# Forget attention: three of its four q and k projection chunks with the weight blocks stationary, a bank per block

## The chip, the cores and the metric

One core of a Trainium2 chip runs the whole program. The metric is the device time of one execution in microseconds (us). A core has a matrix engine (PE), VectorE (DVE), ScalarE (ACT), GpSimd (POOL) and the queues that start transfers (SP among them). Each engine works through its own row of instructions in order; between engines an instruction waits for a semaphore. A matmul multiplies a stationary block, loaded into the array first, with a moving operand of up to 512 columns, and writes into a bank of PSUM (128 partitions by 512 numbers of 32 bits). There are eight banks. ACT and DVE read a bank; when they have read it, it can be used again.

## What is computed

Four layers with different attention, each between two feed-forward layers, and then a second block. The change lies in the second layer's attention alone, the forget attention, over 256 positions with 16 heads of 64:

```
def fox_mixer(x, w_in, b_f, w_out):
    d = MIX_WIDTH                                   # 1024
    q, k, v, f = jnp.split(x @ w_in, [d, 2 * d, 3 * d], axis=-1)
    ...
    log_f = jax.nn.log_sigmoid(f.astype(jnp.float32) + b_f.astype(jnp.float32))
    cum = jnp.transpose(jnp.cumsum(log_f, axis=1), (0, 2, 1))
    o = causal_block_attention(q, k, v, HEAD_DIM ** -0.5, cum)
    return o.reshape(B, S, d) @ w_out

def causal_block_attention(q, k, v, scale, cum=None):
    for i in range(S // Q_BLOCK):                   # two blocks of 128 queries
        lo, hi = i * Q_BLOCK, (i + 1) * Q_BLOCK
        s = jnp.einsum('bqhd,bkhd->bhqk', q[:, lo:hi], k[:, :hi]) * scale
        s = s + cum[:, :, lo:hi, None] - cum[:, :, None, :hi]
        mask = jnp.arange(lo, hi)[:, None] >= jnp.arange(hi)[None, :]
        p = jax.nn.softmax(jnp.where(mask, s, -jnp.inf), axis=-1)
        outs.append(jnp.einsum('bhqk,bkhd->bqhd', p, v[:, :hi]))
```

## The kernel before

The 256 positions are two tiles of 128 (`T` = 0 and 1). Weights come in pieces of 128 by 1024 (512 KB). SP loads a piece into one of five `raw` buffers, ACT rounds it to `whi` (`part_of`, recorded at line 242, where all of ACT's work is recorded), and DVE writes the rest to `wlo` (line 250, where nearly all of DVE's work is recorded). There are eight pairs of `whi` and `wlo`. A product of two 32-bit matrices is made of three matmuls: high by high, high by low, low by high.

A projection can be computed in two ways.

- `Chunk` (three passes, lines 417 to 419): 512 columns of the weights are the moving operand, and a block of the activations (`xt`, already transposed) is stationary. A chunk has four pieces with two blocks of 128 rows each, so for each `T` 24 matmuls of 512 columns go into one bank of the tag `acc`, of which there are two. The four pieces are read for `T` = 0 and again for `T` = 1, and each is given back (`release`) in the second reading.
- `Turned` (lines 426 and 428): a block of 128 by 128 of the weights is stationary, and the activations move. The high part meets both halves of all positions in 512 columns, the low part only the high half in 256 columns, into the bank's upper half. The result is transposed: columns of the weights on partitions, all 256 positions along the row. `whole` drains a bank: ACT copies the upper half to a buffer `h`, and DVE adds the lower half to it. Before, only feed-forward layers use it, two blocks of columns at a time in two banks, with weights in groups of two pieces.

The forget attention (`fox`) needs q and k transposed, with the 64 numbers of a head on partitions. Before, all its projections are a `Chunk`. Per chunk of q or k and per `T`, ACT copies the bank to a natural tile `g` (q scaled by 0.125), PE transposes it in four blocks (`turn8`, line 449, `ps<-ident,g`), and ACT copies the four to another `g`.

The chunks run in this order: q of the first eight heads, two small chunks with v of these heads and the forget gates, k of the first heads; then q and k of the other eight heads, and their v. When the gates are out, `cumsum` makes log-sigmoids on ACT and DVE (buffers `zf`) and sums them over positions with six small matmuls (lines 976 to 985). The attention of the first heads (`attend`) runs as threads beside the later projections, and that of the second heads beside the output projection. For a group of heads: score products (line 701), a bias made of mask and gates on DVE (`h<-mask,cq,pc`), a masked maximum out of the bank (line 713), exponentials on ACT (`wk<-wk,small`), reciprocals and scalings on DVE, four transposes of the weights of attention (line 449, `ps<-ident,wk`), a copy, and value products (line 758).

What stands where on an engine is fixed when the program is built. `Model` keeps an estimated clock for each engine (`run_on`, `pe`), and `tick` starts a step of a thread when the estimate says that it is ready; a scheduler then places the instructions with estimates of its own. On the chip the order does not change, and an instruction whose input is late holds up all that stands behind it on its engine.

## Time and profile before

| what | us |
|---|---|
| median of three runs | 2404.85 (2404.65 to 2406.1) |
| the profiled execution, its own time | 2409.01 |
| its span in the trace | 2407.2 |
| PE busy | 2385.8 |
| DVE busy | 1703.9 |
| ACT busy | 1302.5 |

All times in the trace count from the start of the span. The forget attention's projections lie between about 702 and 789 us, the first changed chunk begins at 728.47, and the next feed-forward layer at 819.45. A matmul's row shows when it began and how long it was in the array; matmuls overlap, so what one costs is the distance between the starts of neighbours. In the rows `ps` is a bank, and `g`, `h`, `wk`, `zf` are buffers of the kinds named above.

### The profile page before, as it was taken

The page shows a single profiled execution, that of the slowest core. Times are in us where ns is not written, and L with a number is a line of the kernel's source. Part 1 is how long each engine was busy: PE and PEld are TensorE (multiplying, and loading weights), DVE is VectorE, ACT ScalarE, POOL GpSimd, SP SyncE. Part 2 cuts the span into 40 slices and gives each one's busy share as a digit, 9 for nine tenths or more (in the row PEclk, how much of TensorE's full clock was granted, in tenths as well). Part 3 has the DMA queues.
Part 4 walks back from the last instruction along what each step waited for, and adds up shares of the span by engine and source line. Part 5 has one row for each costly group of instructions (what it writes and reads, how often), then busy time and mean ns, then how long its engine had stood idle before and what let it go on. Part 6 is the DMA issues. An engine that isn't in the chain of part 4 may idle for free. (4 is left out here: it accounts for less than half of the span.)

```text
span 2407.2 us, 35665 instructions
## 1 busy us (share of the span) xinstructions
PE 2385.8 (99%) x13007; PEld 2010.5 (84%) x13007; DVE 1703.9 (71%) x3265; ACT 1302.5 (54%) x2226; POOL 80.6 (3%) x123
## 2 busy tenths in 40 slices
PE   9999999999999999999999999999999999999998
PEld 7888888888888888888887888888778887888887
DVE  6668876576567866766678877657888767896664
ACT  5555655545456555455475554554655446744553
POOL 0000000000000000000000010000000000000000
PEclk9999999999999999999999999999999999999999
DMA  8555445555656456565454575555545655454552
GB/s 275 195 173 191 156 166 191 178 199 193 201 157 219 154 199 195 176 215 185 130 184 158 196 216 201 189 196 171 185 149 198 201 196 192 158 171 165 195 187 103
DMA packets 126481, 442.81 MB, mean 184 GB/s; under 512 B 14944, under 2 KB 17040, under 8 KB 126304
## 3 DMA queue, kind: packets, MB, share of 16 engines
q1 hardware_dynamic: 117792, 413.49, 51.4%
q0 software_dynamic: 7760, 26.05, 3.6%
q8 instruction: 102, 1.67, 0.3%
q10 hardware_dynamic: 752, 0.98, 0.1%
q14 instruction: 75, 0.61, 0.1%
HBM read 434.14 MB, written 5.80 MB: 183 GB/s over the span
## 5 line engine op out<-in xcount | busy, mean ns | idle before, releaser
L250 DVE TENSOR_TENSOR wlo<-raw,whi 128x1024 fp32r<-128x1024 f32 (+4 forms) x806 | 945.4, 1192 | 237.5 <-ACT whi L242 167.7
L242 ACT ACTIVATE whi<-raw 128x1024 fp32r<-128x1024 f32 (+4 forms) x806 | 821.1, 1031 | 307.2 <-PE ps L419 246.3
L426 PE MATMUL ps<-xt,whi 128*128 128x512 f32 x2496 | 629.1, 392 | 0.7 <-DVE h L250 0.6
L426 PEld LDWEIGHTS ps<-xt,whi 128*128 128x128 f32 x2496 | 451.9, 189 | 85.7 <-DVE h L250 2.9
L428 PEld LDWEIGHTS ps<-xt,wlo 128*128 128x128 f32 x2496 | 342.8, 190 | 25.8
L428 PE MATMUL ps<-xt,wlo 128*128 128x256 f32 x2496 | 350.8, 282 | 0.0
L417 PE MATMUL ps<-whi,g 128*128 128x512 f32 x866 | 339.5, 392 | 0.0
L418 PE MATMUL ps<-wlo,g 128*128 128x512 f32 x866 | 337.7, 390 | 0.0
L419 PE MATMUL ps<-whi,g 128*128 128x512 f32 x866 | 337.0, 389 | 0.0
L417 PE MATMUL ps<-whi,xt 128*128 128x512 f32 (+3 forms) x848 | 329.6, 389 | 4.1 <-ACT whi L242 1.9
L419 PE MATMUL ps<-whi,xt 128*128 128x512 f32 (+3 forms) x848 | 321.1, 379 | 0.6 <-DVE xt L250 0.5
L418 PE MATMUL ps<-wlo,xt 128*128 128x512 f32 (+3 forms) x848 | 319.9, 377 | 0.0
L242 ACT ACTIVATE h<-ps 128x256 f32<-128x256 f32 x352 | 117.4, 376 | 358.4 <-PE ps L428 323.3
L250 DVE TENSOR_TENSOR h<-ps,h 128x256 f32<-128x256 f32 x320 | 122.7, 419 | 218.9 <-ACT h L242 218.5
L419 PEld LDWEIGHTS ps<-whi,g 128*128 128x128 f32 x866 | 162.7, 188 | 34.4 <-DVE g L250 0.4
L417 PEld LDWEIGHTS ps<-whi,g 128*128 128x128 f32 x866 | 162.9, 188 | 31.3
L418 PEld LDWEIGHTS ps<-wlo,g 128*128 128x128 f32 x866 | 163.0, 188 | 30.2
L417 PEld LDWEIGHTS ps<-whi,xt 128*128 128x128 f32 x848 | 159.7, 188 | 32.8 <-ACT whi L242 2.3
L419 PEld LDWEIGHTS ps<-whi,xt 128*128 128x128 f32 x848 | 159.5, 188 | 31.1 <-DVE xt L250 2.0
L418 PEld LDWEIGHTS ps<-wlo,xt 128*128 128x128 f32 x848 | 159.9, 189 | 25.6
L242 ACT ACTIVATE g<-ps 128x512 f32<-128x512 f32 (+6 forms) x192 | 91.8, 492 | 94.7 <-PE ps L419 59.1
L242 ACT ACTIVATE h<-h 128x256 f32<-128x256 f32 x144 | 60.1, 418 | 135.7 <-DVE h L250 135.7
(222 smaller groups left out, 1955.5 us busy)
## 6 DMA issues: line engine op xcount, KB each, us to landing
raw<-in_f SPq DMA_DIRECT2D x526, 512.0 KB, 4.5
raw<-in_ff SPq DMA_DIRECT2D x64, 512.0 KB, 4.6
raw<-in_dsa_qkv SPq DMA_DIRECT2D x48, 512.0 KB, 4.9
raw<-in_w_in SPq DMA_DIRECT2D x40, 512.0 KB, 4.7
raw<-in_wo SPq DMA_DIRECT2D x32, 512.0 KB, 4.4
gb<-in_ln POOLq DMA_DIRECT2D x22, 512.0 KB, 4.7
raw<-in_fox_qk SPq DMA_DIRECT2D x16, 512.0 KB, 5.0
raw<-in_dsa_idx SPq DMA_DIRECT2D x16, 292.0 KB, 3.5
```

The costliest lines, as they stand in the source:

```text
L242: self.pin(self.nc.scalar.activation(out, in_, func, **kw))
L250: self.pin(getattr(self.nc.vector, fn)(out, *a, **kw))
L417: mm(acc, x[0], w[0], start=start, stop=False)
L418: mm(acc, x[0], w[1], start=False, stop=False)
L419: mm(acc, x[1], w[0], start=False, stop=stop)
L426: mm(acc, w, x.rearrange("p z t q->p (z t q)"), start=first, stop=False)
L428: mm(acc[:, S:], w, x[:, 0].rearrange("p t q->p (t q)"), start=False, stop=last)
```

## The change

Three of the four q and k chunks become a `Turned`: k of the first heads, and q and k of the other heads. The first q chunk stays. Each chunk has four blocks of 128 columns. A block has a bank `acc` of its own (where feed-forward layers take two), and its weights are taken in one group of four pieces: eight matmuls of 512 columns with the high parts, then eight of 256 with the low parts. `whole` drains a block into half of a `g` tile, with q's factor 0.125 now in both of its steps. The transposes of these chunks, and ACT's copies around them, are gone. `heads` finds two heads' rows in a block; they lie on partitions as the score product wants them.

```
 class Turned:
-    def __init__(self, m, npieces, kpp, width, x, pairs, post):
+    def __init__(self, m, npieces, kpp, width, x, pairs, post, group=2):
...
-        self.pieces, self.group = [None] * npieces, 2
+        self.pieces, self.group = [None] * npieces, group
...
-            acc = m.ybanks("tr" if j % 2 else "acc")
+            acc = [m.bank("acc")] if len(pair) == 1 else m.ybanks("tr" if j % 2 else "acc")
...
-    def whole(self, out, b, t):
+    def whole(self, out, b, t, scale=1.0):
         half = self.h([P, S])
-        t = self.A(half, b.v[:, S:], AF.Copy, after=t)
-        t = self.V("tensor_tensor", out, b.v[:, :S], half, op=OP.add, after=t)
+        t = self.A(half, b.v[:, S:], AF.Copy, scale=scale, after=t)
+        if scale != 1.0:
+            t = self.V("scalar_tensor_tensor", out, b.v[:, :S], scale, half, op0=OP.mult, op1=OP.add, after=t)
+        else:
+            t = self.V("tensor_tensor", out, b.v[:, :S], half, op=OP.add, after=t)
...
     def heads(self, fut, T, i):
-        l = fut[T]
+        pairs = isinstance(fut, Pairs)
+        l = fut[i // 4] if pairs else fut[T]
...
+            d = slice(64 * (i % 2), 64 * (i % 2) + 64)
+            r.put(l.v[d, i // 2 % 2, T * P:(T + 1) * P] if pairs else l.v[d, i // 2], l.t)
...
+    def turned_chunk(self, xf, kind, dst):
+        tiles = {}
+        def post(c, acc, t):
+            if c % 2 == 0:
+                tiles[c // 2] = self.g([P, 2, S])
+            t = self.whole(tiles[c // 2][:, c % 2], acc[0], t, 0.125 if kind == 0 else 1.0)
+            if c % 2:
+                dst[c // 2].put(tiles[c // 2], t)
+        return Turned(self, 4, 2, 512, lambda T, k: xf[T][k], [(c,) for c in range(4)], post, 4)
...
+        k[0], q[1], k[1] = (Pairs([Later(), Later()]) for _ in range(3))
+        turned = lambda kind, half: self.turned_chunk(xf, kind, (q, k)[kind][half])
...
-        mk(1, 0).both()
+        turned(1, 0).both()
         go(0)
-        mk(0, 1).both()
-        mk(1, 1).both()
+        turned(0, 1).both()
+        turned(1, 1).both()
         go(1)
```

Only this layer's rows change on PE, ACT and DVE; POOL's and SP's stand as before. Lines of the changed kernel are a few higher: 246 for 242, 254 for 250, 430 and 432 for 426 and 428, 456 for 449, 708 for 701, 720 for 713, 765 for 758, 998 to 1007 for 976 to 985.

**First piece.** PE, where the gates' sums stand. Before, they stand in the second q chunk (`ps_1540` is its bank for the first 128 positions):

```order
L417 MATMUL ps_1540_7143<-whi_1511_7027,xt_1437_6702 128x512
L418 MATMUL ps_1540_7143<-wlo_1512_7028,xt_1437_6702 128x512
L419 MATMUL ps_1540_7143<-whi_1511_7027,xt_1437_6702 128x512
L976 MATMUL ps_1543_7175<-zf_1521_7068,h_1456_6772 128x32
L977 MATMUL ps_1543_7175<-zf_1521_7068,h_1456_6772 128x32
L978 MATMUL ps_1543_7175<-zf_1522_7069,h_1456_6772 128x32
L983 MATMUL ps_1544_7180<-h_1456_6772,zf_1521_7068 32x128
L984 MATMUL ps_1544_7180<-h_1456_6772,zf_1521_7068 32x128
L985 MATMUL ps_1544_7180<-h_1456_6772,zf_1522_7069 32x128
L417 MATMUL ps_1540_7143<-whi_1514_7039,xt_1437_6702 128x512
```

Now, on PE, in the third block of the first k chunk (`ps_1527` is that block's bank, `ps_1533` the fourth's):

```order
L430 MATMUL ps_1527_7105<-xt_1437_6702,whi_1500_6961 128x512 x2
L432 MATMUL ps_1527_7105<-xt_1437_6702,wlo_1490_6919 128x256 x2
L432 MATMUL ps_1527_7105<-xt_1437_6702,wlo_1493_6931 128x256
L998 MATMUL ps_1528_7112<-zf_1524_7073,h_1456_6772 128x32
L999 MATMUL ps_1528_7112<-zf_1524_7073,h_1456_6772 128x32
L1000 MATMUL ps_1528_7112<-zf_1525_7074,h_1456_6772 128x32
L1005 MATMUL ps_1529_7117<-h_1456_6772,zf_1524_7073 32x128
L1006 MATMUL ps_1529_7117<-h_1456_6772,zf_1524_7073 32x128
L1007 MATMUL ps_1529_7117<-h_1456_6772,zf_1525_7074 32x128
L432 MATMUL ps_1527_7105<-xt_1437_6702,wlo_1493_6931 128x256
L432 MATMUL ps_1527_7105<-xt_1437_6702,wlo_1498_6950 128x256 x2
```

The gates' six matmuls moved ahead by most of two chunks, to a place behind two blocks and 11 matmuls of the first k chunk.

**Second piece.** DVE around the end of the first k chunk, now (`g_1531` takes the k chunk's third and fourth block, `ps_1527` and `ps_1533`; `ps_1547` is the q chunk's first block; the four `wlo` are weights for the chunk after next):

```order
L254 COPY h_1530_7121<-ps_1529_7117 32x256
L254 TENSOR_TENSOR g_1531_7134<-ps_1527_7105,h_1532_7135 128x256
L254 TENSOR_TENSOR wlo_1536_7152<-raw_1504_7001,whi_1535_7151 128x1024
L254 TENSOR_TENSOR wlo_1539_7160<-raw_1507_7013,whi_1538_7159 128x1024
L254 TENSOR_TENSOR wlo_1542_7168<-raw_1510_7025,whi_1541_7167 128x1024
L254 TENSOR_TENSOR wlo_1545_7176<-raw_1513_7037,whi_1544_7175 128x1024
L254 TENSOR_TENSOR g_1531_7134<-ps_1533_7138,h_1546_7179 128x256
L254 SCALAR_TENSOR_TENSOR g_1552_7207<-ps_1547_7182,h_1553_7208 128x256
L254 SCALAR_TENSOR_TENSOR h_1559_7228<-mask_2_65,cq_1460_6777,pc_1548_7185 128x128
```

Before, banks of q and k were drained by ACT, and on ACT the splits `whi` of the same pieces (`raw_1504` to `raw_1513`) stand singly among the drains:

```order
L242 ACTIVATE whi_1526_7090<-raw_1504_7001 128x1024
L242 ACTIVATE g_1529_7099<-ps_1528_7094 128x512
L242 ACTIVATE whi_1531_7109<-raw_1507_7013 128x1024
L242 ACTIVATE whi_1534_7125<-raw_1510_7025 128x1024
L242 ACTIVATE whi_1537_7137<-raw_1513_7037 128x1024
L242 ACTIVATE g_1539_7141<-ps_1524_7081 128x512
L242 ACTIVATE g_1542_7167<-ps_1541_7162 128x512
```

What moved: the drain of a bank is now a row of DVE too, and the fourth block's drain stands behind all four splits.

**Third piece.** DVE in the first heads' softmax, now (`ps_1554` and `ps_1580` are the second q chunk's second and third block; `wk` are weights of attention):

```order
L254 RECIPROCAL small_1572_7287<-small_1572_7287 128x2
L254 TENSOR_SCALAR wk_1571_7286<-wk_1571_7286,small_1572_7287 128x256 x2
L254 RECIPROCAL small_1576_7304<-small_1576_7304 128x2
L254 SCALAR_TENSOR_TENSOR h_1589_7363<-mask_2_65,cq_1460_6777,pc_1550_7189 128x256
L254 TENSOR_SCALAR wk_1575_7303<-wk_1575_7303,small_1576_7304 128x256 x2
L254 SCALAR_TENSOR_TENSOR g_1552_7207<-ps_1554_7211,h_1579_7320 128x256
L254 SCALAR_TENSOR_TENSOR g_1583_7347<-ps_1580_7323,h_1584_7348 128x256
```

And PE there, now; `ps_1599` is the fourth block, which takes the bank that `ps_1554` had:

```order
L456 MATMUL ps_1595_7387<-ident_1_63,wk_1565_7259 128x128 x4
L456 MATMUL ps_1597_7394<-ident_1_63,wk_1571_7286 128x128 x4
L765 MATMUL ps_1618_7473<-wk_1582_7337,g_1457_6774 64x128
L430 MATMUL ps_1599_7401<-xt_1437_6702,whi_1505_7003 128x512 x2
L430 MATMUL ps_1599_7401<-xt_1437_6702,whi_1508_7015 128x512 x2
```

DVE at the same place before, with the same steps of the softmax:

```order
L250 RECIPROCAL small_1587_7354<-small_1587_7354 128x2
L250 SCALAR_TENSOR_TENSOR h_1593_7376<-mask_2_65,cq_1460_6777,pc_1556_7227 128x256
L250 SCALAR_TENSOR_TENSOR h_1594_7379<-mask_2_65,cq_1460_6777,pc_1557_7229 128x256
L250 RECIPROCAL small_1592_7375<-small_1592_7375 128x2
L250 SCALAR_TENSOR_TENSOR h_1610_7438<-mask_2_65,cq_1460_6777,pc_1558_7231 128x256
L250 TENSOR_SCALAR wk_1591_7374<-wk_1591_7374,small_1592_7375 128x256 x2
L250 TENSOR_TENSOR wlo_1598_7397<-raw_1548_7202,whi_1597_7396 128x1024
```

What moved: two drains of q blocks now stand in DVE's row behind the softmax of two groups, and PE's fourth block needs the first of them; before, DVE drained no projection.

## Rows read from the trace of the kernel before

**Rows 1.** The page, busy time of the engines over the span.
```profile
PE 2385.8 (99%) x13007; PEld 2010.5 (84%) x13007; DVE 1703.9 (71%) x3265; ACT 1302.5 (54%) x2226; POOL 80.6 (3%) x123
```
**Rows 2.** Busy time by stretch: length, then each engine, granted PE clock, DMA.
```profile
10.00:15.00 5.00, 5.00 (x21) 4.02 (x21) 2.49 (x5) 2.03 (x5) 0.00 (x0) 0.70 1.01 412
...
770.00:780.00 10.00, 10.00 (x73) 8.14 (x71) 10.00 (x30) 7.09 (x16) 0.54 (x1) 1.00 0.66 213
...
712.00:789.00 77.00, 75.47 (x484) 63.20 (x484) 55.19 (x155) 52.36 (x112) 4.91 (x9) 1.00 0.64 214
```
**Rows 3.** Waits of PE, 700 to 820 us: total us, times, longest us.
```profile
PE ps L417 <- ACT zf L242: 1.5, 1, 1.5
PE ps L417 <- ACT oth L242: 0.2, 1, 0.2
```
**Rows 4.** PE in order of time, first k chunk: start us, us, what, count.
```profile
728.47 0.40 PE L417 MATMUL ps<-whi,xt 128*128 128x512 f32 x1
...
735.08 0.39 PE L419 MATMUL ps<-whi,xt 128*128 128x512 f32 x1
735.32 0.60 PE L449 MATMUL ps<-ident,g 128*128 128x128 f32 x4
...
735.98 0.40 PE L418 MATMUL ps<-wlo,xt 128*128 128x512 f32 x1
```
**Rows 5.** PE in order of time, a turned chunk of a feed-forward layer.
```profile
656.47 1.98 PE L426 MATMUL ps<-xt,whi 128*128 128x512 f32 x8
658.28 1.12 PE L428 MATMUL ps<-xt,wlo 128*128 128x256 f32 x8
...
667.62 0.40 PE L417 MATMUL ps<-whi,g 128*128 128x512 f32 x1
```
**Rows 6.** The page's groups of a drain's two steps: busy us, mean ns.
```profile
L242 ACT ACTIVATE h<-ps 128x256 f32<-128x256 f32 x352 | 117.4, 376 | 358.4 <-PE ps L428 323.3
L250 DVE TENSOR_TENSOR h<-ps,h 128x256 f32<-128x256 f32 x320 | 122.7, 419 | 218.9 <-ACT h L242 218.5
```
**Rows 7.** PE in order of time, the gates' matmuls and the next row.
```profile
744.44 0.30 PE L976 MATMUL ps<-zf,h 128*128 128x32 f32 x2
...
745.89 0.50 PE L417 MATMUL ps<-whi,xt 128*128 128x512 f32 x1
```
**Rows 8.** DVE in order of time, four splits and the gates' last row.
```profile
727.58 4.63 DVE L250 TENSOR_TENSOR wlo<-raw,whi 128x1024 fp32r<-128x1024 f32 x4 [1.26 <-ACT whi L242]
...
737.16 0.26 DVE L250 SCALAR_TENSOR_TENSOR zf<-zf,zf 128x16 f32<-128x16 f32 x2
```
**Rows 9.** ACT in order of time, a table load in the gates.
```profile
732.59 1.28 ACT L242 ACT_TABLE_LOAD   x1
733.89 0.23 ACT L242 ACTIVATE zf<-zf 128x32 f32<-128x32 f32 x1
```
**Rows 10.** DVE in order of time, the first heads' softmax.
```profile
756.18 1.13 DVE L250 SCALAR_TENSOR_TENSOR h<-mask,cq,pc 128x128 f32<-128x128 f32 x4
...
761.13 0.18 DVE L250 RECIPROCAL small<-small 128x4 f32<-128x4 f32 x1 [1.48 <-ACT wk L242]
...
761.41 0.87 DVE L250 TENSOR_SCALAR wk<-wk,small 128x128 f32<-128x128 f32 x4
762.19 0.28 DVE L713 CUSTOM_DVE_ANT_0 wk<-ps,h 128x128 f32<-128x128 f32 x1
...
762.40 0.88 DVE L250 SCALAR_TENSOR_TENSOR h<-mask,cq,pc 128x256 f32<-128x256 f32 x2
...
764.39 0.42 DVE L713 CUSTOM_DVE_ANT_0 wk<-ps,h 128x256 f32<-128x256 f32 x1
...
765.95 0.61 DVE L250 TENSOR_SCALAR wk<-wk,small 128x256 f32<-128x256 f32 x2
...
770.08 0.69 DVE L250 COPY wk<-ps 128x512 f32<-128x512 f32 x1
```
**Rows 11.** PE in order of time, eight score products, recorded as 16.
```profile
764.73 1.16 PE L701 MATMUL ps<-g,g 64*128 64x128 f32 x16
```

## What I expected before the run

> **What bounds the kernel now.** I read the busy table first: the matrix engine (PE) is busy for 99% of the span [rows 1], so time is won or lost only where PE has less to do or has to wait. Then the stretch that the change touches, from about 712 us to 789 us: PE is busy 75.47 of 77 us, VectorE (DVE) 55.2, ScalarE (ACT) 52.4 [rows 2]. The list of PE's waits from 700 to 820 us has two entries, 1.5 and 0.2 us [rows 3]. The first stands ahead of the changed chunks and is not touched. So in the changed chunks PE waits for nobody. Whatever the change saves on PE is saved, and whatever wait it makes is paid in full, since no later gap can take it back.
>
> **PE's own work.** The three-pass chunk: first starts of 30 matmuls lie 735.08 - 728.47 = 6.61 us apart over 29 steps, 0.228 us each [rows 4]; 48 make 10.94 us. A turned chunk is already there in the feed-forward layers: four blocks from 656.47 to 667.62, 11.15 us, of which eight high passes are 1.81 and so eight low ones 0.98 [rows 5]; one block is 2.79 us. Three chunks: +0.63 us. Removed: six groups of four transposes of q and k. Around one group the starts are 735.98 - 735.08 = 0.90 us apart where two steps would be 0.46 [rows 4]: 0.44 each, -2.64 us in all. Net on PE **-2.0 us**; from -2.6 (blocks cost no more than a chunk) to -0.5 (half of each removed group's 0.44 comes back as restarts at new interruptions of the blocks).
>
> **The drains, and what decides.** Before, a bank held 24 matmuls (5.5 us) and one ACT copy freed it. Now it holds a block of 2.79 us, and is freed by an ACT copy (376 ns) and then a DVE addition (419 ns) [rows 6], about 1.0 us with hand-overs. As sums this is light (DVE +5 us in 77, ACT less than before), and the other engines' idle time hides it. But the two accumulation banks alternate: a bank is wanted again one block after its block has ended, so a drain has 2.79 - 1.0 = 1.8 us of room. **A wait appears wherever more than 1.8 us of other work stands ahead of a drain in ACT's or DVE's queue.** The order shows three kinds of such places. SP's loads and POOL's stand in the same order as before; POOL's forget-gate loads start some 7 us earlier and land ahead of their use.
>
> First, the cumulative gates (first order piece). Before, their six small matmuls stood at 744.44 and took 1.45 us [rows 7], long after their input was ready, the last DVE row at 737.16 + 0.26 [rows 8]. Now they stand inside the third block of the first k chunk: 728.47 + 2 x 2.79 + 1.81 + 3 x 0.12 = 736.2. The input comes no earlier: it hangs on two table loads and small steps on ACT [rows 9], with two block copies put among them in place of one longer copy, so 737.5. PE stands **1.3 us**; 0.5 if the chain is tighter, 2.0 if each copy delays it fully. On ACT, the row after a 1.28 us table load starts 1.30 us after the load did [rows 9]. The Trainium skill (ScalarE: Activation LUTs, What ACT_TABLE_LOAD costs) adds 1.38 us of drain to a load; by that the wait would be 2.8 us longer and the sum below +9.8 instead of +7.0. The row has no such gap, so the row's price stands.
>
> Second, the released weights (second piece). A turned chunk gives its four weight pieces back within its last block, and their splits for the next chunk but one are queued in one lump, ahead of that block's own drain. A split costs 1.16 us on DVE [rows 8]. For the first k chunk: its last block runs from 737.5 + 1.45 + 0.6 = 739.6 to 742.4; DVE may overwrite the first low piece at 741.85, does four splits (4.65) and the addition (0.42), and has freed the bank at 747.0. PE has by then done a q block (2.79) and eight score products (1.1, [rows 11]), and arrives at 746.3. **0.6 us**; between 0 and 1.5, the longest bank wait that the trace has [rows 3].
>
> Third, the softmax (third piece). The drains of q's second and third block stand on DVE behind the whole softmax of the first two groups of heads. DVE from 747.3: 8 biases of 128 (2.1 us), 8 masked-maximum steps of 128 (0.21 each, since the next row starts before one ends, 1.7), 5 biases of 256 (0.4 each, 2.0), 4 steps of 256 (0.35 each in the same way, 1.4), 4 reciprocals (0.4), scalings (1.6 and 1.1), and one idle stretch of 1.5 us for the exponentials [rows 10]: 11.8, then the drain 0.4, so 759.5. PE from 747.0 to the fourth q block has two blocks (5.6), 16 score products (2.2), 12 transposes (1.3, [rows 4]) and one small product: 9.3 us, so 756.3. **3.2 us**, in pieces: some at the transposes of the weights of attention, the rest at the bank. Then the fourth q block's own drain stands behind the second group's softmax and a lump of four splits: on DVE a drain 0.4, four steps 1.4, three biases 1.2, two reciprocals 0.2, a copy 0.65, four scalings 1.1, the splits 4.65, the drain 0.4: 10.0 us [rows 8, 10], so 769.5; PE, with two blocks, eight transposes and eight value products (7.6), wants that bank at 759.5 + 7.6 = 767.1: **2.4 us**. Bounds: 1 to 5 and 0 to 4, since a hand-over or a row's length missed by 0.1 us adds up over some 30 rows.
>
> The last k block's lump meets no such wait: the chunk behind it is the v chunk with 5.5 us to a bank. But by then the second half's scores come 5.5 us later than before, and the attention tail has fewer projection matmuls to lie under; walking it the same way gives waits of 0.65, 0.25 and 1.1 us at its transposes and some tenths at the normalization, 2.4 against 0.2 before. This is the farthest from the rows and I take **1.5**; 0 to 3.
>
> **Sum:** -2.0 + 1.3 + 0.6 + 3.2 + 2.4 + 1.5 = **+7.0 us**. The profiled execution of before is 2409.0 (span 2407.2); the three runs have a median of 2404.85, 4.2 below, so 2416.0 for a profiled execution and 2411.9, say 2412, as a median.
>
> **Rivals.** *The drains keep up* (other side: not slower). The mechanism is the room of 1.8 us: if DVE gets through the first softmax at least 3.2 us faster than in my count, the third kind vanishes, the fourth block's drain comes 3 us earlier, and the tail is as before. For it: the rows were timed while DVE had other work between them. Against it: in 770 to 780 us of before DVE had no idle time at all [rows 2], with no drains in its queue. If the early waits were gone too, -2.0 remain: 2402.9, within the bound of no change. Point of decision: whether q's second block is drained before 756.3.
>
> *Half covered.* The gates and the first lump cost what I say (1.9), the softmax wait is 1 us, the second lump 1 us, the tail nothing: -2.0 + 1.9 + 2.0 = +1.9, 2406.8. For it: the order was made by a planner that put these rows where it expected no wait. Against it: the same planner put the gates' matmuls ahead of their input.
>
> *The clock falls.* With a wait of 1.5 us in it the stretch from 712 to 789 us still has a granted clock of 1.00, the level of 2.4 GHz; only the start shows the lower level of 1.2 GHz, with a mean of 0.70 in 10 to 15 us [rows 2], which is some 1.5 us lost. If each of the two longest waits cost that, 2415. The Trainium skill (TensorE: Matmul & The Clock Gate, Why this matters for your kernels) warns that idle gaps between bursts of matmuls bring the half clock back; no wait of before is long enough to show it here, and my longest single one is 2.4 us.
>
> **How the numbers follow.** What a measurement of this kernel tells from no change is 0.2%, 4.8 us: slower means above 2409.7, faster below 2400.0. Forecast 0.66, clock falls 0.04: slower 0.70. Half covered 0.17, drains keep up 0.09: same 0.26. Faster needs a gain more than twice what PE saves, and no row offers it: 0.04. The bounds of the terms add up to 2403 at the low end (-1.4) and 2420 at the high end (+15); all at one end together is unlikely, and 2404 to 2418 leaves out about 2 in 10, with the best of the rival "drains keep up" at one end.
>
> **What would show it.** No transposes of q and k from the three chunks, and blocks of 2.79 us where PE does not wait. PE's list of waits in the layer: one of about 1.3 us at the first gate matmul, for a DVE row on the gates; waits at the first high pass of q's second and fourth block and of the second k chunk's second block, for a DVE addition out of a bank (0.6, 1, 2.4 us); waits at transposes, for a scaling on DVE (about 2 us together). From there the trace runs some 7 us late and keeps that to the end; the granted clock stays at 1.00. I am wrong if the list of waits is as short as before, or if DVE reaches the drain of q's second block before PE asks for the bank.

## The result, and the profile after

The changed kernel takes 2417.55 us (median of 5; 2414.95 to 2418.75), the kernel before, beside it on the same chip, 2404.78 (median of 5). The ratio is 1.0052, 95% interval 1.0040 to 1.0063: slower, by about 12.8 us where I had forecast 7. The time lies inside the range and on the side I had expected; the size is nearly double.

The profiled execution of the changed kernel took 2414.95 us, with a span of 2413.1, only 5.9 us above the one of before (span 2407.2). So the two traces differ by less than the medians. For one part, the profiled execution of the changed kernel was the fastest of its five, 2.6 us below their median. The larger part is in the trace of before, and has nothing to do with the change: that execution began badly. PE in order of time, first at the start of the kernel before, then of the kernel after (start us, us, engine, line, operation, count; in brackets the idle time before the row and what ended it):

```profile
9.21 1.28 PE L417 MATMUL ps<-whi,xt 128*128 128x512 f32 x2 [1.95 <-ACT whi L242]
...
13.06 0.48 PE L418 MATMUL ps<-wlo,xt 128*128 128x512 f32 x1
```
```profile
7.42 0.99 PE L421 MATMUL ps<-whi,xt 128*128 128x512 f32 x2 [0.26 <-ACT whi L246]
...
9.78 0.48 PE L422 MATMUL ps<-wlo,xt 128*128 128x512 f32 x1
```

The same instructions are 3.28 us later in before (a longer wait, then matmuls 0.43 us apart instead of 0.23). A second piece lies ahead of the first changed chunk, where the order of all instructions is still the same in both kernels. ACT in order of time, before and after:

```profile
724.00 1.06 ACT L242 ACTIVATE whi<-raw 128x1024 fp32r<-128x1024 f32 x1 [1.81 <-PE ps L419]
724.97 0.36 ACT L242 ACTIVATE g<-ps 128x256 f32<-128x256 f32 x1
```
```profile
719.10 1.06 ACT L246 ACTIVATE whi<-raw 128x1024 fp32r<-128x1024 f32 x1 [0.24 <-DMA raw<-in_fox_qk]
720.07 0.36 ACT L246 ACTIVATE g<-ps 128x256 f32<-128x256 f32 x1
```

In both a split of a weight stands ahead of a drain. In the execution of before its weight came late from the DMA (it landed at 723.90; PE, which the profile names, had finished before), so the drain was late, and PE stood the 1.5 us of [rows 3]; the two starts there are 1.82 us apart in before and 0.42 after. Before the first changed matmul the two traces have therefore drifted 4.9 us apart: 728.47 [rows 4] against 723.57. Only what follows belongs to the change. From there to the next feed-forward layer before takes 819.45 - 728.47 = 90.98 us, and after 826.21 - 723.57 = 102.64: **+11.7 us**, close to the 12.8 of the medians. Over the whole forget-attention layer, from its first chunk's first matmul (701.86 and 698.38), it is 117.59 against 127.83, +10.2, because before had the late DMA in it. PE's rows at both ends of the layer, after:

```profile
698.38 0.39 PE L421 MATMUL ps<-whi,xt 128*128 128x512 f32 x1
...
826.21 0.40 PE L421 MATMUL ps<-whi,xt 128*128 128x512 f32 x1
```

Behind the layer the distance between the traces stays as it is to the end (6.8 us at 826, 6.0 at 2032). L421 to L423 are the three passes now; the other lines have the numbers given with the change. The page's busy time answers to [rows 1]:

```profile
PE 2387.4 (99%) x13031; PEld 2011.2 (83%) x13031; DVE 1708.5 (71%) x3277; ACT 1301.0 (54%) x2226; POOL 80.8 (3%) x123
```

DVE has the 12 additions more, and otherwise nothing in this line shows a loss. PE's list of waits in the layer does (total us, times, longest us); of before it had two entries [rows 3]:

```profile
PE ps L456 <- DVE wk L254: 3.3, 3, 1.8
PE ps L430 <- DVE g L254: 1.9, 3, 1.2
PE ps L998 <- DVE zf L254: 1.1, 1, 1.1
PE ps L430 <- ACT zf L246: 0.4, 1, 0.4
PE ps L708 <- DVE small L720: 0.2, 1, 0.2
```

These are 6.9 us, and the layer lost more. A list of waits begins a wait where the last matmul's modelled end is; distances between starts miss nothing. PE in order of time, through the gates and then from q's second block to the second k chunk:

```profile
731.62 0.51 PE L432 MATMUL ps<-xt,wlo 128*128 128x256 f32 x3
733.24 0.41 PE L998 MATMUL ps<-zf,h 128*128 128x32 f32 x2 [1.10 <-DVE zf L254]
...
747.06 2.00 PE L430 MATMUL ps<-xt,whi 128*128 128x512 f32 x8
750.19 0.92 PE L456 MATMUL ps<-ident,wk 128*128 128x128 f32 x4 [1.13 <-DVE wk L254]
750.87 1.20 PE L432 MATMUL ps<-xt,wlo 128*128 128x256 f32 x8
751.99 1.16 PE L708 MATMUL ps<-g,g 64*128 64x128 f32 x16
753.09 0.90 PE L456 MATMUL ps<-ident,wk 128*128 128x128 f32 x4
755.77 0.70 PE L456 MATMUL ps<-ident,wk 128*128 128x128 f32 x4 [1.78 <-DVE wk L254]
756.40 0.69 PE L765 MATMUL ps<-wk,g 128*64 128x128 f32 x2
757.28 3.17 PE L430 MATMUL ps<-xt,whi 128*128 128x512 f32 x8 [0.20 <-DVE g L254]
760.29 1.10 PE L432 MATMUL ps<-xt,wlo 128*128 128x256 f32 x8
761.23 2.00 PE L430 MATMUL ps<-xt,whi 128*128 128x512 f32 x8
763.07 1.11 PE L432 MATMUL ps<-xt,wlo 128*128 128x256 f32 x8
764.03 0.60 PE L456 MATMUL ps<-ident,wk 128*128 128x128 f32 x4
...
766.16 0.43 PE L765 MATMUL ps<-wk,g 128*64 128x128 f32 x2
767.75 0.50 PE L430 MATMUL ps<-xt,whi 128*128 128x512 f32 x1 [1.17 <-DVE g L254]
```

Two things are to be seen. An undisturbed block takes 764.03 - 761.23 = 2.80 us, as forecast. And the block at 757.28 takes 3.95: its eight high passes need 760.29 - 757.28 = 3.01 us where the next block's need 1.84. The granted clock says why (us; then length, PE, PEld, DVE, ACT, POOL, granted clock, DMA):

```profile
752.00:756.00 4.00, 2.22 (x23) 1.78 (x23) 3.93 (x19) 3.00 (x13) 1.15 (x2) 1.00 0.21 65
756.00:760.00 4.00, 3.80 (x13) 2.63 (x12) 3.78 (x14) 1.79 (x6) 0.54 (x1) 0.57 0.24 67
```

For most of four microseconds PE had the lower level, 1.2 GHz. To add it all up, I counted PE's instructions of each kind in each stretch and multiplied by the distance of undisturbed starts (0.230 a high pass, 0.119 a low one, 0.228 one of the three passes, 0.089 a transpose, 0.069 and 0.064 the recorded score and value products, the gates 0.12 each). What a stretch takes beyond that is lost:

| stretch of after, us | what lies in it | lost | the prediction's term |
|---|---|---|---|
| 723.6 to 738.3 | first k chunk, gates | 2.1 | 1.3 |
| 738.3 to 747.1 | q's first block, scores | 1.0 | 0.6 |
| 747.1 to 757.3 | q's second and third block, softmax | 5.1 | 3.2 |
| 757.3 to 761.2 | q's fourth block, low clock | 1.2 | none |
| 761.2 to 779.1 | second k chunk | 2.8 | 2.4 |
| 779.1 to 826.2 | v chunk, rest of the attention, output | 5.1 | 1.5 above before |

That is 17.3 us over the whole way; before lost 4.2 on its own, most of it behind 756 us. The undisturbed work fell from 86.8 to 85.3 us. So: -1.5 + 17.3 - 4.2 = +11.6.

### The profile page after: what moved, and what is told of

The parts are those of the page before. It is cut to its first block, busy times and chain, and to the rows that moved or that the text cites. A ratio compares the mean times of both kernels' runs of the same rounds, so it can differ in the third digit from the quotient of the medians.

```text
span 2413.1 us, 35728 instructions
## 1 busy us (share of the span) xinstructions
PE 2387.4 (99%) x13031; PEld 2011.2 (83%) x13031; DVE 1708.5 (71%) x3277; ACT 1301.0 (54%) x2226; POOL 80.8 (3%) x123
## 5 line engine op out<-in xcount | busy, mean ns | idle before, releaser
L430 PE MATMUL ps<-xt,whi 128*128 128x512 f32 x2592 | 655.2, 393 | 3.4 <-DVE g L254 1.9
L430 PEld LDWEIGHTS ps<-xt,whi 128*128 128x128 f32 x2592 | 469.6, 189 | 92.4 <-DVE h L254 2.8
L432 PEld LDWEIGHTS ps<-xt,wlo 128*128 128x128 f32 x2592 | 355.8, 190 | 27.0 <-issue 0.4
L432 PE MATMUL ps<-xt,wlo 128*128 128x256 f32 x2592 | 364.5, 282 | 0.0
L421 PE MATMUL ps<-whi,g 128*128 128x512 f32 x866 | 339.3, 392 | 0.0
L423 PE MATMUL ps<-whi,g 128*128 128x512 f32 x866 | 336.8, 389 | 0.0
L421 PE MATMUL ps<-whi,xt 128*128 128x512 f32 (+3 forms) x800 | 308.9, 386 | 1.0 <-ACT xt L246 0.6
L423 PE MATMUL ps<-whi,xt 128*128 128x512 f32 (+3 forms) x800 | 301.6, 378 | 0.5 <-DVE xt L254 0.5
L422 PE MATMUL ps<-wlo,xt 128*128 128x512 f32 (+3 forms) x800 | 300.8, 376 | 0.0
L423 PEld LDWEIGHTS ps<-whi,g 128*128 128x128 f32 x866 | 162.7, 188 | 34.4 <-DVE g L254 0.4
L421 PEld LDWEIGHTS ps<-whi,g 128*128 128x128 f32 x866 | 162.9, 188 | 31.3
L423 PEld LDWEIGHTS ps<-whi,xt 128*128 128x128 f32 x800 | 150.2, 188 | 28.6 <-DVE xt L254 1.8
L421 PEld LDWEIGHTS ps<-whi,xt 128*128 128x128 f32 x800 | 150.3, 188 | 28.1 <-ACT xt L246 1.6
L422 PEld LDWEIGHTS ps<-wlo,xt 128*128 128x128 f32 x800 | 150.6, 188 | 24.0
L246 ACT ACTIVATE g<-ps 128x512 f32<-128x512 f32 (+7 forms) x180 | 85.3, 487 | 91.8 <-PE ps L423 59.3
```

The lines of the kernel that those rows point to most:

```text
L246: self.pin(self.nc.scalar.activation(out, in_, func, **kw))
L421: mm(acc, x[0], w[0], start=start, stop=False)
L422: mm(acc, x[0], w[1], start=False, stop=False)
L423: mm(acc, x[1], w[0], start=False, stop=stop)
L430: mm(acc, w, x.rearrange("p z t q->p (z t q)"), start=first, stop=False)
L432: mm(acc[:, S:], w, x[:, 0].rearrange("p t q->p (t q)"), start=False, stop=last)
```

## The experiments

Each run is the changed kernel with the further edit that is shown. Two lengths are used: from the first k chunk to the next feed-forward layer (90.98 before, 102.64 after), and the whole layer (117.59, 127.83). PE's wait ahead of the first k chunk, where the order is the same in the first eight runs, came out at up to 1.1 us, so a length is good to about 1 us. The whole layer of before holds its late DMA, some 1.4 us; the shorter length does not. Ratios are to the kernel before on the same chip. Where an edit adds lines, the line numbers of its rows are higher; the tiles tell what a row is.

| kernel | ratio (95%) | whole layer, us |
|---|---|---|
| before | 1 | 117.6 |
| all three turned (the change) | 1.0052 (1.0040 to 1.0063) | 127.8 |
| first k chunk alone | 1.0016 (1.0006 to 1.0026) | 120.5 |
| second q chunk alone | 1.0002 (0.9992 to 1.0011) | 117.0 |
| second k chunk alone | 1.0004 (0.9995 to 1.0014) | 118.4 |
| gates' rows from elsewhere | 1.0050 (1.0035 to 1.0065) | 126.4 |
| dummy matmuls in the waits | 1.0050 (1.0035 to 1.0065) | 127.3 |
| transposes held back | 1.0049 (1.0034 to 1.0064) | 126.7 |
| drain ahead of the splits | 1.0037 (1.0024 to 1.0050) | 124.7 |
| three edits | 1.0038 (1.0025 to 1.0050) | 124.8 |
| gates ahead | 1.0046 (1.0031 to 1.0061) | 126.2 |
| gates ahead, drain ahead | 1.0040 (1.0025 to 1.0055) | 125.7 |
| drained by ACT alone | 1.0028 (1.0018 to 1.0038) | 123.8 |
| products summed in the bank | 1.0006 (0.9997 to 1.0016) | 119.7 |

**One chunk at a time.** The edit, here for the first k chunk; the other two in the same way:

```diff
-        k[0], q[1], k[1] = (Pairs([Later(), Later()]) for _ in range(3))
+        k[0] = Pairs([Later(), Later()])
...
-        turned(0, 1).both()
-        turned(1, 1).both()
+        mk(0, 1).both()
+        mk(1, 1).both()
```

> Only the first k chunk is turned; the second q and k chunks stay three-pass. The measure in all expectations is the stretch of the layer from the first matmul of its first k chunk to the first matmul of the next feed-forward layer: 90.98 us before, 102.64 us with all three chunks turned (+11.7). Theory of the prediction (drains and gates): PE's own work -0.7, a wait of about 1.3 us at the cumulative gates' first matmul, and nothing else, because the bank of the fourth block is wanted only 5.5 us later and the q and k drains are ACT copies again: +0.6, 91.6 us, granted clock 1.00. Rival (each turned block costs more than its 2.79 us, by restarts at interruptions; a third of the unexplained cost): +2 us or more, 93 us, with no single long wait. Rival (clock): a wait of 1.3 us at the gates brings the low clock behind it: a slice with a clock of 0.6, +1.8, 92.8 us.

Measured: 94.35 us, not the theory's 91.6. In number it is the first rival's "+2 us or more", but that one had no single long wait, and here there are two. The gates' wait is there (last row), and one that I had not expected, at the transposes of the weights of attention (first row); the middle row is the late bank ahead of the changed chunk. The clock was 1.00 throughout, so the rival of the clock falls for this kernel. PE's waits:

```profile
PE ps L456 <- DVE wk L254: 1.2, 1, 1.2
PE ps L421 <- ACT zf L246: 1.1, 1, 1.1
PE ps L998 <- DVE zf L254: 1.0, 1, 1.0
```

> Only the second q chunk is turned. Theory of the prediction: PE's own work -0.7; the gates' matmuls stand in its second block, long after their input: no wait; the drains of its blocks wait on DVE behind splits, but the softmax comes only after the chunk (the order has the first score products behind it), so the softmax finds three-pass banks: at most 0.5 us of bank waits: 90.98 - 0.7 + 0.5 = 90.8 us. Rival (the waits come from the softmax having too little PE work to lie under once 8 transposes and copies are gone, whoever is turned): waits at the transposes of the weights of attention of 1 us or more: 92 us or more. Rival (restarts in turned blocks): 92 us with no wait over 0.5 us.

Measured: 91.82, between the two. One wait of 1.25 us is new, at transposes, but of a tile `g` of the k chunk and not of the weights of attention: PE waits for a bank that a copy on DVE (`wk`) has yet to empty. It is neither the theory's bank wait of 0.5 us nor the rival's place.

```profile
776.66 0.66 PE L456 MATMUL ps<-ident,g 128*128 128x128 f32 x4 [1.25 <-DVE wk L254]
```

> Only the second k chunk is turned; it is the chunk that runs beside the first softmax here. Theory of the prediction (drains behind the softmax and behind split lumps on DVE): bank waits and waits at the transposes of the weights of attention, as for q in the full change but later: -0.7 + 3 = +2.3, 93.3 us, the waits named as DVE rows (an addition out of a bank, a scaling). Rival (DVE stood 1.7 us for the cumulative gates read back from DRAM, because the gates now lie close ahead of the score products; the drains are harmless): here the gates stand some 10 us ahead of the score products, so no such stand and no waits at the transposes: 90.3 us.

Measured: 92.79. The chunk that runs beside the softmax has four waits of 0.2 to 0.3 us, one at a bank and three at transposes, named as the theory said; the theory had 93.3, its rival 90.3.

From the first k chunk on, the three add up to +3.4 + 0.8 + 1.8 = 6.0 us (by the ratios 0.22%, 5.3 us); together they cost 11.7 (0.52%, 12.5 us). So no single chunk makes the loss, and about half of it comes only when they are together. Turned together they bring the first score products forward, from 54.7 us after the layer's start to 42.8, and, as I read it, the softmax then meets blocks on both sides whose drains also want DVE.

**The gates' round trip through DRAM.** The trace after has something I had ruled out. DVE in order of time, the first biases:

```profile
744.04 0.35 DVE L254 SCALAR_TENSOR_TENSOR h<-mask,cq,pc 128x128 f32<-128x128 f32 x1 [0.39 <-DMA pc<-ckd]
745.69 0.61 DVE L254 SCALAR_TENSOR_TENSOR h<-mask,cq,pc 128x128 f32<-128x128 f32 x2 [1.30 <-DMA pc<-ckd]
```

The rows of gates, written to DRAM and read back, land up to 7.3 us after their issue, while the DMA engines moved 307 and 407 GB/s in all (740 to 744 and 744 to 748 us). The run that loads such rows from a weight array instead:

```diff
-            nc.gpsimd.dma_start(ckd, ck[:32])
...
-                src = ckd[8 * half + 2 * pr:8 * half + 2 * pr + 2]
-                nc.gpsimd.dma_start(t, bass.AP(src.tensor, src.offset, [[0, P], [S, 2], [1, S]]))
+                src = self.ap["wo"][0, 0]
+                nc.gpsimd.dma_start(t, bass.AP(src.tensor, src.offset + 1024 * (8 * half + 2 * pr), [[0, P], [1024, 2], [1, S]]))
```

> All three chunks turned; the rows of cumulative gates that the biases of the softmax read are loaded from a weight array instead of from the DRAM copy of the gates, and that copy is not written, so these loads wait for nothing (the values of the attention are others for it). In the trace with the change DVE stands 0.39 and 1.30 us at the first biases for these loads. Theory of the prediction (DVE's queue of drains, splits and softmax makes the waits): DVE has other rows to do and the waits at the transposes (1.13 and 1.78 us) stay within 0.5 us: 102 to 102.6 us. Rival (the round trip of the gates through DRAM starts the softmax late): the two waits at the transposes fall by about 1.7 us together, and if the low clock behind them goes too, by 1.2 more: 99.7 to 101 us.

Measured: 100.32 us from the first k chunk, in the rival's range, but this execution had a bank wait of 1.05 us ahead of that chunk; over the whole layer it gained 1.4 us, and the kernel's ratio is the same. The first wait at the transposes went, the second stayed at 1.70, and so did the low clock. The stand for the gates' rows is real, worth 1.4 to 2.3 us by these two lengths (the ratio does not show so little), and not the cause of the rest.

**The low clock.** Dummy matmuls ahead of the two groups of transposes:

```diff
     def transposes(self, srcs, fill=0):
         b = self.bank("tr")
+        for _ in range(fill):
+            self.nc.tensor.matmul(b.v, self.xt[:, 0, 0, 0], self.xt[:, 0].rearrange("p z t q->p (z t q)"), start=True, stop=True)
...
```

> The full change, with dummy matmuls (4 and 7 of 128x512, whose results are overwritten) on PE directly ahead of the two groups of transposes at which PE stood 1.13 and 1.78 us. They take 0.9 and 1.6 us, so PE multiplies where it stood and reaches the same places at the same time. In the trace with the change the granted clock is 0.57 in 756 to 760 us and the eight high passes behind the second wait take 3.01 us instead of 1.84. Theory (the waits bring the low clock): no low clock there, the eight high passes take 1.84 us, the layer from its first k chunk takes 101.4 us instead of 102.64. Rival (the low clock has another cause, or belongs to that execution alone): the passes take 3.0 us again, 102.6 us, up to 0.3 more where the dummies outlast the wait.

Measured: the clock stayed up, and 101.66 is close to the 101.4 of the theory. But the two bank waits behind it grew, from 0.20 and 1.17 to 0.91 and 1.74 us, and the kernel's time did not move. PE's rows behind the second filling, then the clock:

```profile
759.57 2.12 PE L430 MATMUL ps<-xt,whi 128*128 128x512 f32 x8 [0.91 <-DVE g L254]
761.53 1.11 PE L432 MATMUL ps<-xt,wlo 128*128 128x256 f32 x8
...
769.58 0.72 PE L430 MATMUL ps<-xt,whi 128*128 128x512 f32 x2 [1.74 <-DVE g L254]
```
```profile
756.00:760.00 4.00, 3.03 (x15) 2.03 (x15) 3.93 (x17) 2.24 (x8) 0.54 (x2) 1.00 0.43 127
```

The eight high passes take 1.96 us instead of 3.01, and PE arrives early at a bank that DVE has not yet drained: 1.05 us saved, 0.71 + 0.57 given back. The low clock cost almost nothing, because PE was not what set the pace there.

**Later transposes.** The planner is told that the scaled weights are 2 us later:

```diff
-                yield lambda e=e: max(ready[e], self.can("tr"))
+                yield lambda e=e: max(ready[e] + hold, self.can("tr"))
...
```

> The full change; in the forget attention alone the planner is told that scaled weights of attention are ready 2 us later than it reckons, so it puts their transposes later among PE's blocks. Theory A (PE's order asks for the weights of attention before DVE and ACT have them; the work to lie under is there, in the wrong place): the waits at the transposes, 2.9 us, the low clock behind them, 1.2, and some restarts go: 98 to 99 us. Theory B (the one of the prediction: drains queued on DVE behind the softmax): the drains stay where they are, so the wait moves to the banks: 101.5 to 102.6 us.

Measured: 101.16, below the range of B by a little and far above that of A. No wait at transposes is left, and the waits stand at the banks:

```profile
PE ps L430 <- DVE g L254: 3.2, 3, 1.9
PE ps L708 <- DVE small L720: 2.4, 2, 2.0
PE ps L998 <- DVE zf L254: 1.1, 1, 1.1
```

Where PE stands is a matter of its order; how long, of DVE's queue.

**Drains ahead of the splits.**

```diff
-                        if part and last_pair:
-                            m.release(p)
                         if part and i == n - 1:
                             self.post(j, acc, m.pe_done())
+                        if part and last_pair and len(pair) > 1:
+                            m.release(p)
+                        elif part and last_pair and i == n - 1:
+                            for r in self.pieces:
+                                m.release(r)
```

> The full change, but in the turned blocks the weight pieces are given back after the last block's drain has been issued, so that the drain stands ahead of the lump of four splits on DVE and ACT. Theory of the prediction (a drain behind four splits): the bank waits of 0.52 us (second q block) and 1.17 us (second block of the second k chunk) go, with their restarts: 100.5 to 101 us. Rival (the lump is not the limit; the weights split later are awaited instead): a new wait for a split of a weight, or the same bank waits: 102.6 us or more.

Measured: 99.69, a gain of 3.0 us where 1.6 to 2.1 was expected. Both bank waits of the lumps are gone from the list, as the theory said; 1.93 us for a scaling and 1.26 for an ACT copy, both at transposes, remain. The granted clock is 1.00 throughout here, so part of the gain may be the low clock's 1.2 us, and not the lumps'.

```profile
PE ps L459 <- DVE wk L257: 2.6, 3, 1.9
PE ps L459 <- ACT wk L249: 1.3, 1, 1.3
PE ps L1001 <- DVE zf L257: 1.1, 1, 1.1
```

**Three edits together** (this one, the later transposes, and the gates' matmuls 2 us later in the planner's reckoning):

```diff
                 t = V("scalar_tensor_tensor", f[:, :16], z[:, T], 0.0, l[:, T], op0=OP.min, op1=OP.subtract)
-            yield t
+            yield t + 2000.0
             mm = nc.tensor.matmul
```

> The full change with three edits together: drains ahead of the lumps of splits, the transposes of the weights of attention 2 us later in the planner's reckoning, and the cumulative gates' matmuls 2 us later. Theory (waits from the order, not from the blocks themselves): the gates' wait (1.3 with its restart), the lumps' (1.7 to 2.0), the transposes' with the low clock (4 to 5) go: 102.64 - 7.5 = 95 us or less, some 4 us above before, and the whole kernel within 0.3% of before. Rival (single-bank blocks and groups of four cost the time themselves, by restarts and by interruptions): 99 us or more.

Measured: 99.16: a miss for the theory that the order alone is to blame. It is the rival's number, but not for the rival's reason, since the time still goes into waits. The gates' wait is gone, but the gates' rows then come later too, DVE stands 3.6 us for them, and PE has a bank wait of 2.48 us and 1.41 at score products.

**The gates ahead.** The layer's two chunks with the values and the gates run before its first q chunk, and each hop of the gates' chain is put 3 us earlier:

```diff
-        self.start(mk(0, 0), vf[0])
-        vf[1].both()
+        self.start(*vf)
+        mk(0, 0).both()
...
-            yield t
+            yield t - 3000.0
...
```

> The full change, with the gates' chain moved ahead: the layer's first two chunks (values and gates) run before its first q chunk, and the chain of small steps is put 3 us earlier at each hop in the planner's reckoning, so the gates' matmuls stand in the q chunk, some 18 us ahead of the first score products instead of 7. The computation is the same. Measure here: the whole forget-attention layer, from its first chunk's first matmul to the next feed-forward layer's: 117.59 us before, 127.83 with the change. Theory G (the gates' chain starts the softmax late): PE's wait at the gates goes (1.1, with its restart 1.5), DVE no longer stands 1.7 us for the gates read back from DRAM, so the waits at the transposes fall by as much and the low clock behind them may go (1.2): 123 to 124.7 us. Theory Q (queues of drains, splits and softmax on DVE alone): only the gates' own wait goes: 126.3 us.

Measured: 126.2 for the layer, the number of Q, but by another way. The gates' own wait, which was to go, has only moved into the q chunk (1.12 us). DVE no longer waits for the gates' rows at all; the first wait at the transposes went, and the second is 1.78 as before.

The same with the drains ahead of the splits, as in the earlier diff:

> The gates' chain moved ahead and the drains issued ahead of the lumps of splits, all three chunks turned, nothing left out. If the two causes are separate, their savings add: 1.5 + 1.7 + 1.2 for the gates, 3.1 for the lumps (127.83 - 124.72 in the run with that edit alone): 120 to 121 us, still 2 to 3 us above before. If DVE's softmax and drains are the limit of this stretch anyway, the second saving is lost again: 123.5 us or more.

Measured: 125.7. The savings do not add; the second case holds (123.5 us or more). Part of it is a low clock of its own, behind the gates' wait, in which three-pass matmuls start 0.43 us apart:

```profile
724.00:728.00 4.00, 3.70 (x18) 3.03 (x19) 1.98 (x6) 1.10 (x2) 0.52 (x1) 0.78 0.61 164
728.00:732.00 4.00, 4.00 (x18) 3.15 (x17) 2.34 (x2) 1.83 (x3) 1.44 (x3) 0.79 0.66 215
```

**Drains taken off DVE.** A block is drained by one ACT copy:

```diff
-            t = self.whole(tiles[c // 2][:, c % 2], acc[0], t, 0.125 if kind == 0 else 1.0)
+            t = self.A(tiles[c // 2][:, c % 2], acc[0].v[:, :S], AF.Copy, scale=0.125 if kind == 0 else 1.0, after=t)
+            self.free(acc[0], t)
```

> The full change, but a turned block is drained by one ACT copy of its first half, and the second half (the low half of x by the high half of the weights) is not added: the output lacks that part. DVE has 12 additions of 0.42 us less, 5 us, and a bank is free one hop after its block. Theory Q (drains queued on DVE): the bank waits of 0.52, 0.20 and 1.17 us go, and the softmax on DVE is up to 1.2 us earlier (three drains stand ahead of its last weights): 124 to 126 us for the layer. Theory G (the gates' chain): 127 us or more, because the gates' wait and DVE's wait for their rows stay.

Measured: 123.8 for the layer, just under the range of Q, 4.1 us less than with the change, the largest gain of a single edit so far (ratio 1.0028). The three bank waits for DVE are gone; 1.21 for an ACT drain, 1.56 at transposes and 1.45 at the gates are left. It also changes the planner's order, so the gain is not the additions' alone.

**The products summed in the bank.** To see whether a full kernel can have that, all three products of a block are added up in the same 256 columns:

```diff
+                        w = m.cols(p, k * 512 + c * P, P)[part]
+                        for z in range(2 - part):
+                            mm(acc, w, m.xt[:, kt, z].rearrange("p t q->p (t q)"), start=part == 0 and z == 0 and kt == 0, stop=part == 1 and kt == 7)
...
+            t = self.A(d, b.v.rearrange("p (a s)->p a s", s=S), AF.Copy, scale=0.125 if kind == 0 else 1.0, after=t)
```

> All three chunks turned, nothing left out, in another form: all three products of a block are summed in the same 256 columns of a bank (24 matmuls of 256 columns instead of 8 of 512 and 8 of 256), so two blocks share one bank, a bank is wanted again 5.9 us after it was filled, and one ACT copy of 512 columns drains it, with no addition on DVE; the weight pieces are given back behind that copy, and the gates' matmuls stand 2 us later. PE's own work: eight low passes of 256 columns take 0.95 to 0.98 us in the trace, so 24 are 2.9 and twelve blocks 35.1 us, against 32.8 for three chunks and 2.6 for the removed transposes: -0.3. Theory Q (single-bank blocks, whose drains stand in DVE's queue, make the loss): waits of 0.5 us or less remain beyond those of before, the forget-attention layer takes 117 to 118.5 us (before 117.59, with the change 127.83), the kernel is within 0.2% of before. Rival (turned blocks bring the softmax forward and PE asks for its results too early, however they are drained): waits of 1 us or more at the transposes of the weights of attention, 121 us or more.

Measured: 119.65 for the layer and 1.0006 (0.9997 to 1.0016) for the kernel: 8.2 of the 10.2 us are back, and it can't be told from before. The layer lies between the 118.5 of Q and the 121 of its rival. No wait at a bank is left, and an undisturbed block takes 2.88 us as reckoned. One wait of 2.06 us remains at transposes, the rival's sign and more than the theory allowed. Ahead of it DVE stood 5.2 us for the gates' rows: PE's waits, then DVE's entry for these rows (6.1 us with one later stand).

```profile
PE ps L488 <- DVE wk L286: 2.1, 1, 2.1
PE ps L1027 <- DVE zf L286: 0.3, 1, 0.3
```
```profile
DVE h L286 <- DMA pc<-ckd: 6.1, 5, 1.9
```

This run changes four things at once (where the sums stand, the engine of the drain, the splits behind it, the later gates), so the 8.2 us are not the drains' alone.

No version of the kernel ran faster than before: at most 2 us of PE's work are to be had, and none of these layouts kept the softmax under cover as well as three-pass chunks do.

## Why the prediction was right, and where its size was off

**The rule held, in part.** PE waits for DVE, as forecast, and the bank waits stand where the rule puts them: 0.52, 0.20 and 1.17 us. The lumps' waits went when the drain stood ahead of the splits (3.1 us of the layer), and drains on ACT alone gave back 4.1. But "more than 1.8 us of other work ahead of a drain makes a wait" covers only these 1.9 us of the list; 3.3 stand at transposes, for the softmax itself. So of a loss of 10 to 12 us about 4 are shown to be the drains on DVE, in a run whose order changed with the edit. That they make most of it is likely from the sums in the bank (8.2), which changed other things too, and not shown. The rival of blocks that cost more by themselves falls: an undisturbed block is 2.80 us.

**PE's own work.** -2.0 forecast, -1.5 by count of the undisturbed work. The difference lies in the removed transposes: the forecast's 0.44 us a group holds a restart, the count's 4 x 0.089 does not, and restarts came back in other places. Two bounds were added up wrongly: half of 2.64 coming back gives -0.7 at the upper end, not -0.5, and the low ends of all terms give -1.1, not -1.4. Neither decides anything here.

**First, the gates.** 1.3 forecast. Three low passes and the wait take 733.24 - 731.62 = 1.62 us, of which 0.36 are passes: 1.26. The chunk lost 0.5 more at its second block, whose bank still held the last values and gates (the ACT entry of 0.4 in the list), a wait that I had not looked for. The row's price of a table load [rows 9] was right: in the trace after, too, the row behind each of the two loads starts 1.29 us after the load did. The Trainium skill (ScalarE: Activation LUTs, What ACT_TABLE_LOAD costs) adds a drain of 1.38 us to each, which this wait, with two loads ahead of it, does not show. That side sum of the prediction, 2.8 us more, was no real test: the 737.5 was read off the same chain in before, and would have held such drains already.

**Second, the first lump.** 0.6 forecast, 0.52 listed at 742.85, 1.0 lost in the stretch.

**Third, the softmax.** This is the term that was mis-sized: 3.2 forecast, 5.1 measured. The list of waits gives 1.13 + 1.78 + 0.20 = 3.1, which looks right and is not: the other 2.0 lie in rows between the waits, for instance the four transposes at 753.09, which have no bracket in front and last 0.90 us where an undisturbed four (764.03) last 0.60. One step under the term was wrong outright: "POOL's forget-gate loads start some 7 us earlier and land ahead of their use". They landed late, DVE stood 1.7 us, and two runs without that stand gained 1.4 and 1.6 us of the layer. That is nearly all of the error: from its first bias (743.04) until q's second block was drained (757.2) DVE took 14.1 us, where the forecast had 12.2 (747.3 to 759.5). Of the 4.6 us between the sum of 7.0 and the 11.6, this term has 1.9, the low clock 1.2 and the gates' chunk 0.8. I put most of the wait at the bank; it came at the transposes, which only says that the planner put PE's queue that way (the run with later transposes has it at the banks). Between 743.04 and 756.81 DVE's row holds no drain and no split, so what held PE at the transposes was the softmax itself with that stand, and not a drain ahead of it. DVE in order of time, q's second and third drain:

```profile
756.28 0.61 DVE L254 TENSOR_SCALAR wk<-wk,small 128x256 f32<-128x256 f32 x2
756.81 0.75 DVE L254 SCALAR_TENSOR_TENSOR g<-ps,h 128x256 f32<-128x256 f32 x2
```

Both stand behind all the scalings, as forecast. But the point of decision did not go clearly my way. Its 756.3 was counted in the trace of before; from the first k chunk's start PE was to ask for the bank after 27.8 us and to get it after 31.0, and it asked after 33.5 (757.08) and got it after 33.7. DVE had begun that drain at 756.81, 0.3 us before PE asked. By the letter that is my sign of being wrong; PE came so late only because it had stood at the transposes for the same row of DVE.

**The second lump.** 2.4 forecast; the list has 1.17 at 767.75, the start distances 1.59 - 0.13 = 1.5 there and 2.8 in the whole chunk. DVE in order of time, that drain:

```profile
767.27 0.43 DVE L254 SCALAR_TENSOR_TENSOR g<-ps,h 128x256 f32<-128x256 f32 x1
```

Counted from the start of q's fourth block (757.28 here, 759.5 in the forecast), DVE was done with it after 10.4 us, where 10.0 was forecast. PE asked after 9.3 instead of 7.6, and 1.2 of that is the low clock. So the wait is short because PE was late, not because DVE was early; with the clock up (dummies) it was 1.74.

**The tail.** 1.5 forecast; 5.1 lost against about 3 in before from its v chunk on (769.45), so about 2. The list names only 0.55, and with what is around them these two waits cost 0.96. The rest is spread over steps of under 0.25 us each; what makes them is not settled.

**The clock.** I had given the fall of the clock 4 in 100, and expected 1.00 throughout, because the wait of 1.5 us in before had brought no fall. It fell to 0.57 behind waits of 1.13 and 1.78. It is no answer for the size, though: with it filled away the time stayed.

**The medians.** 7.0 was reckoned on the profiled execution of before and shifted to the median. That was sound; the comparison of the two profiled executions (+5.9) would have misled.

## What to carry to other kernels

A bank that holds half the work must be drained in half the time, by engines whose queue holds everything else: before splitting accumulation into smaller blocks, write down what stands ahead of each drain, or sum so that one copy on a less busy engine drains it. Three edits that cost 3.4, 0.8 and 1.8 us alone cost 11.7 together here; as I read it, because together they moved one long chain, the softmax, into the way of the drains. Compare the distance between starts of the same instructions in both traces, from the last point where the orders agree: it showed 4.9 us that were not the change's, and 5 us or more that no list of waits had.

## What I had not expected of the hardware

The lower clock came in the middle of a busy layer: behind waits of 1.13 and 1.78 us with the change, 1.70 (gates' rows from elsewhere), 1.96 (later transposes), 1.78 (gates ahead), 1.12 (gates and drain ahead) and 2.06 (sums in the bank), each time for a few microseconds. It stayed away behind 1.5 us in before [rows 3], behind 1.74 in the run with dummies, and behind 1.93 and even 2.48 us in the runs with drains ahead and with three edits. The two runs with the gates ahead have the same wait of 1.12 us at the gates' matmuls: behind it the clock stayed at 1.00 in one, and fell to 0.78 and 0.79 (slices of 4 us) in the other. PE's busy time and the clock in the run with three edits:

```profile
752.00:756.00 4.00, 2.32 (x22) 1.89 (x22) 4.00 (x20) 3.02 (x10) 0.39 (x1) 1.00 0.00 0
756.00:760.00 4.00, 2.56 (x14) 2.22 (x15) 4.00 (x14) 4.00 (x9) 0.68 (x2) 1.00 0.53 154
```

The Trainium skill (TensorE: Matmul & The Clock Gate, Why this matters for your kernels) warns of idle gaps between bursts. The run with dummies agrees as far as it goes: with the waits at the two transposes filled (0.50 us of them was left), the clock stayed up. But PE still stood 0.91 and 1.74 us behind them there, and the length of a wait does not tell whether the clock falls here.

The other surprise is how far one execution can stray where nothing differs: 3.3 us in the first 13 us, and 1.5 us from one late load.
